# Hybrid encoder trunk on one core: zero-filled 128-row second score product in chunked attention, latent attention's chunk mask as four contraction rows, and a new layout for the experts' last third

## The chip, the cores and the metric

The kernel runs on one core of one Trainium2 chip. The metric is device time in microseconds for one execution of the whole program; the time before is the median of 3 runs. TensorE is called PE, VectorE DVE, ScalarE ACT, GpSimd POOL and SyncE SP.

## The reference, cut to what matters

Two layers on 512 tokens of width 1024, all in float32. Each layer mixes four branches (a state space scan, forgetting attention "fox", latent attention "mla", chunked attention "chk"), then a dense feed-forward (layer 0) or top-2-of-8 experts (layer 1), then a gated side input.

```
# mla: a query sees all keys of its own and earlier chunks of 64
mask = (kpos // 64) <= (qpos // 64)
s = where(mask, q @ k, -inf); prob = softmax(s)          # q, k: 64 plain + 32 rotary columns per head
# chk: own chunk and 8 chunks before it, plus a bias by clipped relative position
s = q @ k + bias; prob = softmax(s)                       # 64 columns per head
# experts: for each token the two best of 8
y = (silu(x @ w1[e]) * (x @ w3[e])) @ w2[e]               # 1024 -> 1408 -> 1024
```

## The kernel before, in words

Most products keep float32 precision by splitting each operand into a high and a low part: three PE products (hi·hi, hi·lo, lo·hi; lines 157 to 159, called L15x below) take the place of one. Weights are fetched by SP, split by ACT (line 137) and DVE (line 139), and used.

In the two mixers a planner orders the instructions of each engine by its own model of costs: large gate products (`gates`) fill PE while the softmax chains of the attention units run on DVE and ACT. Each unit does two heads `a`, and for each head four blocks `b` of 128 queries against n = 128(b+1) keys (`attention`, line 580): the score products (line 587), for fox a mask product of bf16 (line 589), for mla a mask product of one row (line 591), then maximum, exponential, scaling (lines 598 to 601), transposes (line 604) and products with the values (line 616). Tiles of one tag share a number of buffers; a new tile takes any that has come free.

- chk (`unit_chk`): `dq` holds a head's query, high part in its own 64 rows and low part in the other 64; `dk` holds the key's high part in both halves. Their product over 128 rows gives hi·hi + lo·hi. The second product, `dl` (the key's low part, 64 rows) with the high half of `dq`, adds hi·lo. This pair is issued 8 times for each n over two layers, two units and two heads, 32 in all.
- mla (`unit_mla`): the query `mq` and key `mk` are plain float32 tiles of 96 rows; each score product is two PE passes. Blocks mask the last 64 keys for the first 64 queries with the one-row product (32 of these). Four products of 64 rows (line 840) per layer add a low part of the query projection: 8 in all. POOL copies the rotary key into `mk` (line 855).
- s5_prep, between the two chk units, gives POOL a long chain of small operations (lines 357 to 448); POOL also adds the gated branches into `A` (line 669).

The experts (`moe`) have an order written out by hand for PE, ACT and DVE. Each expert has up to 128 rows in part A and the rest in part B. A works on split weights (`cut`, lines 1304 and 1306; products on line 1353). B uses the raw float32 weights with the rows as the stationary operand (line 1357); it is behind two branches on the count (lines 1491 and 1494): 64 rows, 32 rows or none. Weights come in 35 pieces an expert: up 0 to 27 in thirds i = 0, 1, 2 (the last third is 384 wide, the others 512), down in between and at 28 to 34. For 32 rows and i < 2, `quads` splits a piece's columns into four groups of 32 array columns that run side by side; for i = 2 only two groups run. `evac` gates a third, `turn` transposes it, `put` stores a part's output. Before the last expert stands a branch (line 1714) over `extras`, which holds a loop for experts with more than 192 rows.

## Time and profile before

| what | value |
|---|---|
| median of 3 runs | 2002.85 us (1998.05 to 2003.78) |
| profiled execution | 2003.2 us, span 2001.4 us |
[...]
| PE busy | 1941.3 us (97%) |
| DVE, ACT, POOL busy | 1191.4, 908.8, 315.6 us |
| DMA | 309.23 MB |

The span is from the first to the last instruction; 1.8 us of the profiled execution lie around it. A busy PE includes time in which a product's tail runs while nothing new is streamed, so what an edit on PE is worth is read from the starts of successive products and not from the busy share. A timeline row gives start, duration, engine, line, operation, tiles and shape (contraction rows * stationary columns, then rows x streamed columns), and in brackets the idle time ahead of it.

### The profile page before, as it was taken

What the parts mean: (1) busy time and instruction counts of PE and PEld (TensorE: products, weight loads), DVE (VectorE), ACT (ScalarE), POOL (GpSimd) and SP (SyncE); (2) the same over time, 40 slices, a digit from 0 to 9 for tenths busy, and PEclk for the clock granted to TensorE, in tenths of its full rate; (3) what the DMA queues carried; (4) which work ended last, traced back from release to release, by engine and by line L of the source; (5) the groups of instructions that cost most, each with busy time, mean ns of one, the idle gap of its engine ahead of it and who ended that gap; (6) DMA issues with size and microseconds to landing.
All of it is one profiled execution on the core that took longest, in us unless ns stands there. A gap on an engine that the chain in (4) does not pass through costs nothing. (4 is left out here: it accounts for less than half of the span.)

```text
span 2001.4 us, 27201 instructions
## 1 busy us (share of the span) xinstructions
PE 1941.3 (97%) x9922; PEld 1522.6 (76%) x9922; DVE 1191.4 (60%) x1849; ACT 908.8 (45%) x1345; POOL 315.6 (16%) x616
## 2 busy tenths in 40 slices
PE   7999999999999999999999999999999999999998
PEld 7787776788888888888777776887677877666567
DVE  5867564744333333345667564745899986566574
ACT  5535434333322223255435434333678776555454
POOL 1058020220000000001068020220100000000011
PEclk9999999999999999999999999999999999999999
DMA  5332223224433333323332223135699995858542
GB/s 170 119 107 85 75 89 132 67 92 159 147 95 95 102 98 90 111 89 110 99 106 85 76 89 132 53 112 213 230 365 373 372 353 214 299 205 316 198 156 106
DMA packets 94563, 309.23 MB, mean 155 GB/s; under 512 B 12161, under 2 KB 15105, under 8 KB 94402
## 3 DMA queue, kind: packets, MB, share of 16 engines
q1 hardware_dynamic: 89218, 289.40, 42.1%
q0 software_dynamic: 5040, 17.44, 2.6%
q8 instruction: 99, 1.62, 0.3%
q14 instruction: 62, 0.51, 0.1%
q10 hardware_dynamic: 144, 0.26, 0.0%
HBM read 283.46 MB, written 23.60 MB: 153 GB/s over the span
## 5 line engine op out<-in xcount | busy, mean ns | idle before, releaser
L137 ACT ACTIVATE whi<-wraw 128x1024 fp32r<-128x1024 f32 (+2 forms) x211 | 217.5, 1033 | 465.7 <-PE a L158 268.1
L139 DVE TENSOR_TENSOR wlo<-wraw,whi 128x1024 fp32r<-128x1024 f32 (+2 forms) x211 | 258.1, 1229 | 284.7 <-ACT whi L137 275.9
L158 PE MATMUL a<-hT_lo,whi 128*128 128x512 f32 (+3 forms) x1056 | 412.1, 391 | 0.8 <-DVE hT_lo L163 0.7
L159 PE MATMUL a<-hT_hi,wlo 128*128 128x512 f32 (+3 forms) x1056 | 412.5, 391 | 0.3 <-DVE wlo L139 0.3
L157 PE MATMUL a<-hT_hi,whi 128*128 128x512 f32 (+3 forms) x1056 | 411.8, 391 | 0.7 <-ACT hT_hi L163 0.7
L1306 DVE TENSOR_TENSOR wlo<-raw,whi 128x1024 fp32r<-128x1024 f32 (+1 forms) x198 | 228.0, 1160 | 52.3 <-ACT whi L1304 43.0
L159 PEld LDWEIGHTS a<-hT_hi,wlo 128*128 128x128 f32 (+1 forms) x1056 | 197.2, 187 | 42.8 <-issue 3.5
L158 PEld LDWEIGHTS a<-hT_lo,whi 128*128 128x128 f32 (+1 forms) x1056 | 197.5, 187 | 41.9 <-DVE hT_lo L163 1.9
L157 PEld LDWEIGHTS a<-hT_hi,whi 128*128 128x128 f32 (+1 forms) x1056 | 197.0, 187 | 41.6 <-issue 1.8
L1304 ACT ACTIVATE whi<-raw 128x1024 fp32r<-128x1024 f32 (+1 forms) x198 | 198.8, 1008 | 57.1 <-PE a L1353 39.5
L669 POOL TENSOR_TENSOR A<-A,t 128x512 f32<-128x512 f32 x48 | 78.2, 1660 | 262.3 <-DVE t L668 262.3
L157 PE MATMUL a<-whi,hT_hi 128*128 128x256 f32 (+2 forms) x328 | 110.6, 337 | 1.0 <-ACT hT_hi L163 1.0
L159 PE MATMUL a<-whi,hT_lo 128*128 128x256 f32 (+2 forms) x328 | 109.2, 334 | 0.3
L158 PE MATMUL a<-wlo,hT_hi 128*128 128x256 f32 (+2 forms) x328 | 108.8, 332 | 0.0
L1353 PE MATMUL a<-whi,heA_hi 128*128 128x512 f32 (+1 forms) x304 | 93.2, 388 | 9.5 <-PEq L1714 3.5
L1353 PE MATMUL a<-whi,heA_lo 128*128 128x512 f32 (+1 forms) x304 | 90.7, 379 | 0.0
L1353 PE MATMUL a<-wlo,heA_hi 128*128 128x512 f32 (+1 forms) x304 | 90.5, 378 | 0.0
L1353 PEld LDWEIGHTS a<-whi,heA_hi 128*128 128x128 f32 x304 | 54.4, 189 | 28.2 <-issue 13.9
L157 PEld LDWEIGHTS a<-whi,hT_hi 128*128 128x128 f32 x328 | 62.7, 191 | 7.3 <-ACT hT_hi L163 1.5
L159 PEld LDWEIGHTS a<-whi,hT_lo 128*128 128x128 f32 x328 | 62.7, 191 | 6.2 <-DVE hT_lo L163 0.9
L1306 DVE TENSOR_TENSOR r_lo<-raw,r_hi 128x1024 fp32r<-128x1024 f32 (+1 forms) x50 | 57.4, 1148 | 16.3 <-ACT r_hi L1304 13.9
L599 ACT ACTIVATE P<-b,mx 128x128 f32<-128x128 f32 (+1 forms) x64 | 33.7, 527 | 72.7 <-DVE mx L598 72.2
(529 smaller groups left out, 3562.5 us busy)
## 6 DMA issues: line engine op xcount, KB each, us to landing
raw<-in_moe_w13a SPq DMA_DIRECT2D x113, 512.0 KB, 7.3
raw<-in_moe_w SPq DMA_DIRECT2D x74, 512.0 KB, 8.1
wraw<-in_w_gate SPq DMA_DIRECT2D x64, 512.0 KB, 3.6
wraw<-in_ffn_w SPq DMA_DIRECT2D x64, 512.0 KB, 3.6
raw<-in_moe_w13b SPq DMA_DIRECT2D x61, 384.0 KB, 6.2
wraw<-in_w_in_T SPq DMA_DIRECT2D x20, 512.0 KB, 3.8
wraw<-in_w_branch SPq DMA_DIRECT2D x16, 512.0 KB, 3.7
wraw<-in_w_o SPq DMA_DIRECT2D x16, 512.0 KB, 3.6
```

Of the source, the lines that this page charges most:

```text
L137: act(hi[:, :n], raw[:, :n], AF.Copy)
L139: tt(out=lo[:, :n], in0=raw[:, :n], in1=hi[:, :n].bitcast(F), op=OP.subtract)
L157: mm(o, a[0], b[0], start=start, stop=False)
L158: mm(o, a[0], b[1], start=False, stop=False)
L159: mm(o, a[1], b[0], start=False, stop=stop)
L599: act(P[:, :n], src[:, :n], AF.Exp, bias=mx[:, 0:1], accum_out=mx[:, 1:2])
L669: gtt(out=A[m], in0=A[m], in1=g[m], op=OP.add)
L1304: act(hi[:, :w], raw[:, :w], AF.Copy)
L1306: return tt(out=lo[:, :w], in0=raw[:, :w], in1=hi[:, :w].bitcast(F), op=OP.subtract)
L1353: mm(dst[x][:, :w_], st[sa][:, k, :], w[:, cs[x]], start=first and q == 0, stop=last and q == 2)
```

## The change

The chk low key becomes one 128-row tile per head, zero in the half that faces the query's low part; the second product runs over 128 rows. POOL fills the zeros. The mla mask becomes four more contraction rows (96 to 100), loaded from a small table by POOL's DMA queue; the mask product and its two constant tiles go. The 64-row product in the mla projection runs over 128 rows. A pad takes the place of the constant tiles; another one of 128 bytes a partition is put in the router's pool.

In the experts `quads` holds for i = 2 too, which needs w2's rows of the last third in another order (set on the host), a gating in two pieces for the other row counts (`ordered`) and another transpose for 32 rows. Expert 6 does all of its last B pieces (28 to 34) ahead of A's 32 to 34. Its stores move from POOL's queue to SP's, and the DMAs of `extras` from SP's to POOL's.

```diff
-                    mm(s[:, :n], qT[:, qs], kT[:, :n], start=(i == 0), stop=(kind == "chk" and i == len(qk) - 1))
+                    mm(s[:, :n], qT[:, qs], kT[:, :n], start=(i == 0), stop=(kind != "fox" and i == len(qk) - 1))
-                if kind == "mla":
-                    mm(s[:, n - 64:n], half_b, neg_b, start=False, stop=True)
...
-                q2 = [qk_tile(cp, f"dq{a}", 9) for a in range(2)]
+                q2 = [qk_tile(cp, f"dq{a}", 10) for a in range(2)]
...
-                kl = qk_tile(cp, "dl", 9)
+                kl = [qk_tile(cp, f"dl{a}", 10) for a in range(2)]
+                for a in range(2):
+                    nc.gpsimd.memset(kl[a][halves(a)[1]].bitcast(F), 0.0)
...
-                        marks.append(tt(out=kl[own], in0=ps[own], in1=k2[a][own].bitcast(F), op=OP.subtract))
+                        marks.append(tt(out=kl[a][own], in0=ps[own], in1=k2[a][own].bitcast(F), op=OP.subtract))
...
-                    qks.append([(q2[a], k2[a]), (q2[a][own], kl[own])])
+                    qks.append([(q2[a], k2[a]), (q2[a], kl[a])])
...
+                for a in range(2):
+                    nc.gpsimd.dma_start(out=qs[a][96:100], in_=I["mla_mask"][0])
+                    nc.gpsimd.dma_start(out=ks[a][96:100], in_=I["mla_mask"][1])
...
-                    mm(ps, wuq[1][0:64, 1, ws], cqb[0:64], start=False, stop=True)
+                    mm(ps, wuq[1][:, 1, ws], cqb, start=False, stop=True)
...
-                attention(ap, "mla", [[(qs[a][0:96], ks[a][0:96])] for a in range(2)], V, (2 * pr, 2 * pr + 1), yps)
+                attention(ap, "mla", [[(qs[a][0:100], ks[a][0:100])] for a in range(2)], V, (2 * pr, 2 * pr + 1), yps)
...
-            return m == 32 and i < 2
+            return m == 32
...
+        def ordered(out, in0, in1):
+            a0, a1 = (x.rearrange("p (a b) -> p a b", a=2) for x in (in0, in1))
+            for q, lo, hi in ((out[:, 0:256], 0, 128), (out[:, 256:384], 128, 192)):
+                tt(out=q.rearrange("p (a b) -> p a b", a=2), in0=a0[:, :, lo:hi], in1=a1[:, :, lo:hi], op=OP.mult)
...
+            if quads(m, i) and i == 2:
+                for f, (c0, c1) in enumerate(((0, 128), (128, 192), (64, 192))):
+                    nc.tensor.transpose(bank[0:c1 - c0, f * 64:(f + 1) * 64], t_[0][0:64, c0:c1], ident[0:64, 0:64])
+                act(g[:, 0:2, 0:32], bank[:, 0:64].rearrange("p (k q) -> p k q", k=2), AF.Copy)
+                act(g[0:64, 2, 0:32], bank[0:64, 64:96], AF.Copy)
+                act(g[64:128, 2, 0:32], bank[64:128, 160:192], AF.Copy)
+                return
...
-            B(28, 32, 2)
+            ahead = er is None and e == NE - 2
+            B(28, 35 if ahead else 32, 2)
             A(32, 33, 34)
             if er is None and not last:
-                put(yd[e * 128:(e + 1) * 128, :], 128, nc.gpsimd if e == NE - 2 else nc.sync)
-            B(32, 35)
+                put(yd[e * 128:(e + 1) * 128, :], 128, nc.sync)
+            if not ahead:
+                B(32, 35)
...
+    blk = np.arange(S)[None, :] // 64 - 2 * np.arange(4)[:, None]
+    o["mla_mask"] = C(np.stack([blk == 0, NEG * (blk == 1)]).astype(np.float32))
```

## Rows read from the trace of the kernel before

**Rows 1.** The page, part 1: busy time of each engine.

```profile
PE 1941.3 (97%) x9922; PEld 1522.6 (76%) x9922; DVE 1191.4 (60%) x1849; ACT 908.8 (45%) x1345; POOL 315.6 (16%) x616
```

**Rows 2.** Waits of PE: us in total, times, longest.

```profile
PE b L604 <- DVE P L601: 7.9, 11, 1.8
```

**Rows 3.** Busy time by stretch, experts 4 to 6.

```profile
1640.00:1850.00 210.00, 207.92 (x1331) 142.87 (x1329) 134.03 (x135) 120.97 (x149) 5.13 (x5) 1.00 0.71 261
```

**Rows 4.** Timeline of PE, a chk block of 512 keys.

```profile
76.72 0.49 PE L604 MATMUL b<-cst,P 128*128 128x128 f32 x3
...
77.37 0.50 PE L587 MATMUL b<-dl,dq 64*128 64x512 f32 x1
77.80 0.50 PE L159 MATMUL a<-hT_hi,wlo 128*128 128x512 f32 x1
78.13 0.40 PE L157 MATMUL a<-hT_hi,whi 128*128 128x512 f32 x1
```

**Rows 5.** Timeline of PE, a fox block of 512 keys.

```profile
193.21 0.55 PE L604 MATMUL b<-cst,P 128*128 128x128 f32 x3
...
193.83 0.40 PE L587 MATMUL b<-f1s,f0s 128*128 128x512 f32 x1
194.07 0.23 PE L589 MATMUL b<-caus_b,ident_b 128*128 128x128 bf16 x1
...
194.43 0.40 PE L159 MATMUL a<-hT_hi,wlo 128*128 128x512 f32 x1
```

**Rows 6.** Timeline of PE, mla blocks and the gate products behind one.

```profile
277.94 0.49 PE L587 MATMUL b<-mk,mq 96*128 96x128 f32 x2
...
288.10 1.02 PE L587 MATMUL b<-mk,mq 96*128 96x512 f32 x2
289.05 0.20 PE L591 MATMUL b<-neg_b,half_b 1*128 1x64 bf16 x1
289.18 0.50 PE L158 MATMUL a<-hT_lo,whi 128*128 128x512 f32 x1
289.52 0.40 PE L159 MATMUL a<-hT_hi,wlo 128*128 128x512 f32 x1
...
292.49 0.39 PE L157 MATMUL a<-hT_hi,whi 128*128 128x512 f32 x1
```

**Rows 7.** Timeline of PE, the mla projection around line 840.

```profile
275.66 0.39 PE L839 MATMUL a<-cqb,whi 128*128 128x512 f32 x1
...
276.74 0.39 PE L158 MATMUL a<-cqa,whi 128*128 128x512 f32 x1
```

**Rows 8.** Part B, 32 rows: group of i = 2, then timeline, a piece of i = 0.

```profile
L1357 PE MATMUL b<-raw,yh 128*32 128x384 f32 x64 | 10.7, 488 | 0.0
...
1641.40 3.66 PE L1357 MATMUL b<-raw,yh 128*32 128x256 f32 x64
```

**Rows 9.** PE's branches: timeline, lines 1494 and 1714, and what waited.

```profile
1677.99 5.36 PE L1357 MATMUL b<-raw,yh 128*32 128x384 f32 x32
...
L1494 PEldq COMPARE_BRANCH  x1: 179/179/179, 1680.0 to 1680.0; - x1
...
L1714 PEldq COMPARE_BRANCH  x1: 4372/4372/4372, 1847.9 to 1847.9; - x1
...
1852.62 0.70 PE L1353 MATMUL a<-whi,heA_hi 128*128 128x512 f32 x2 [3.49 <-PEq L1714]
```

**Rows 10.** POOL: timeline, then a DMA's issue (ns) and landing (us).

```profile
118.39 0.46 POOL L359 TENSOR_TENSOR Qr<-gp,gp 128x128 f32<-128x128 f32 x1 [56.99 <-PE b L376]
...
261.87 11.03 POOL L669 TENSOR_TENSOR A<-A,t 128x512 f32<-128x512 f32 x8 [58.42 <-DVE t L668]
...
289.19 1.28 POOL L855 COPY mk<-krot 32x512 f32<-32x512 f32 x2 [14.08 <-DVE wlo L139]
...
L410 POOL DMA_DIRECT2D s5d<-Qr x4: 601/632/827, 128.8 to 1050.0; - x4
...
s5d<-Qr POOLq DMA_DIRECT2D x4, 256.0 KB, 2.4
```

## The prediction

> **What bounds the kernel now.** I read the page's first part, then the waits of PE, then the busy time by stretch, then PE's timeline around each place that the change touches. The first shows PE busy for 97% of the span [rows 1]; the reader is to see that no other engine passes 60%. A busy share alone doesn't say that PE is the limit, so the second view is needed: in the attention blocks PE's transposes wait for the softmax chain in 11 places only, 7.9 us in all [rows 2], and there are 96 such blocks (three kinds, two layers, two units, two heads, four blocks). In 85 of 96 the chain is ready before PE comes to it. The third view says the same of experts 4 to 6, where part B runs: PE is busy 207.92 of 210 us at a DMA share of 0.71 [rows 3]. So in the stretches that the change edits, time taken from PE is time taken from the span, if nothing new is waited for. The timelines then say how much there is to take: the distance from the start of one product to the start of the next is what a product costs.

> **The unit of account.** In a run of gate products of 128 rows and 512 columns, 13 distances take 292.49 - 289.52 = 2.97 us, so one product costs 0.228 us [rows 6].

> **chk's second product, 32 of them.** In the block of 512 keys the 64-row product takes 0.43 us to the next start and the gate product behind it 0.33 [rows 4]. Two products at 0.228 would be 0.46, so 0.30 us is lost where the array goes from 64 rows back to 128. The whole sequence, transposes to the second gate product, is 78.13 - 76.72 = 1.41 us. The fox block has the same transposes, two score products of 512 columns and a mask product besides, and takes 194.43 - 193.21 = 1.22 [rows 5]; there the second score product has 128 rows and costs 0.24. So chk's pair after the change can't well cost more than fox's with its mask: the saving is at least 0.19 a block. At most it is 0.40: the 0.30 above and 0.10 for the first product, if it too gets rid of what the switch to 64 rows costs it. I take 0.33, near the upper end, since fox's remainder holds a mask product that chk hasn't got. Blocks of 256 and 384 keys repeat the pattern; those of 128 are so short that loading the weights may set their pace, and for them I take 0.25 between 0.1 and 0.33, an estimate. Sum: 24 x 0.33 + 8 x 0.25 = 9.9 us (5.4 to 12.2).

> The wider product itself costs nothing more: the time goes by columns streamed, 0.24 us for fox's 128 rows against 0.43 for these 64 [rows 4, 5].

> **mla's mask, 32 of them.** Two score passes of 512 columns, the mask and the gate product behind it take 289.52 - 288.10 = 1.42 us; the mask's own distance is 0.13, the gate product's 0.34 instead of 0.228 [rows 6]. After the change two passes and a gate product are left. Plain float32 goes at 5.36 us for 16 turns of 384 columns on part B [rows 9], 0.87 ns a column, so the two passes are 0.89 and the sum 1.12: 0.30 us saved. If the product of 100 rows still delays its 128-row neighbour, only the mask and the 0.11 behind it go: 0.24. If the passes run without any gap, 0.34. In 6 of the 32 the mask stands behind value products and only its own 0.13 goes. Sum: 26 x 0.30 + 6 x 0.13 = 8.6 us (7.0 to 9.6).

> No row here has 100 rows, and the nearest, 96, leaves open whether it counts as the full array. [...]

> **The projection, 8 products.** From the product ahead of the 64-row one to the second behind it is 276.74 - 275.66 = 1.08 us for three [rows 7], against 3 x 0.228 = 0.69. Full 128 rows give back 0.39 each, 3.1 us in all; as with chk I keep half as the lower bound (1.6 to 3.2).

> **Experts, last third with 32 rows.** The group of i = 2 holds 64 instructions of 384 columns, 10.7 us [rows 8], in bunches of 32 [rows 9]: two experts, 5.36 us each. In four groups of columns there will be 64 instructions of 192. A bunch of 64 with 256 columns takes 3.66 us [rows 8]; if columns set that, 192 take 2.75 and 2.6 us are saved, if the number of instructions does, 3.66 and 1.7. Since 32 instructions of 384 and 64 of 256 cost the same by the column and group (0.87 and 0.89 ns), columns set it. Two experts: 5.2, less 0.2 for wider transposes, 5.0 us (3.4 to 5.2). The two more copies on ACT and the second gating operation on DVE have pieces 28 to 31 of B and A between them and their reader; without that cover they would cost under 1 us an expert.

> **Expert 6's order.** PE's branch over `extras` takes 4.37 us from 1847.9, and the first product of expert 7 has been waited for 3.49 us [rows 9]: little array work was queued ahead of it, B's last 24 short products. After the change A's 18 products of 0.228 us, 4.1 us, stand ahead. Does PE's sequencer run that far ahead? At 1680.0 it is at a branch while the bunch in the array goes on to 1677.99 + 5.36 = 1683.35 [rows 9]: 3.3 us, or some 20 products of 5.36 / 32. So most of the 4.37 is covered; I take 2.8 us saved (0 to 3.5).

> [...]

> **What is added, and what covers it.** POOL's eight zero fills: no row has this shape; the nearest are the addition of 1.4 us on 128 x 512 (11.03 / 8) and nothing [rows 10]. In the second chk unit a fill waits until the first head of the first unit has read its query, since its buffer comes free there; behind it on POOL is s5_prep's chain, which stands still anyway, 57 us up to 118.39 [rows 10]. That new tiles take whatever buffer is free shows in mla: both copies into the second unit's keys run together at 289.19, right behind the first head's last scores, the second head's still to come [rows 6, 10]. I take 0; without the cover 8 x 1.4 = 11 us.

> The mask rows are four DMAs a unit on POOL, 0.63 us to issue and 2.4 to land [rows 10]. At worst they queue behind the additions that end at 261.87 + 11.03 = 272.90: issued by 275.4, landed by 277.8, the rotary copies done by 276.7, beside a first score at 277.94 [rows 6, 10]. I take 0; if the score comes a microsecond earlier, under 1 us a layer. POOL waits 58 us ahead of those additions, so the DMAs can go long before. SP's two stores of expert 6 hold up the fetches of expert 7 by ACT's and DVE's copies, a microsecond or two, and 18 buffers are ahead; POOL, whose gathers of the last expert stand behind these stores, is freed of issuing them. The loads of `extras` aren't run: expert 7's first product follows the branch. The pads issue nothing.

> **Sum.** The mixers give 9.9 + 8.6 + 3.1 = 21.6 us, of which I count nine tenths, 85 blocks of 96 not waiting for the chain: 19.4. The experts give 5.0 + 2.8 = 7.8. Together 27.2 us, against the profiled 2003.2 us (span 2001.4 and 1.8 around it): 1976.0; from the median, 2002.85, which is 0.35 below: 1975.7. I predict 1976 us, own range 1969 (33.7 saved, every upper bound) to 1987 (16 saved: 14.0 x 0.9 + 3.4). Less than 0.3%, 6 us, can't be told from no change.

> **Rivals.**
> - The lost time belongs to the change of kind (transposes, scores, gates) and not to the number of rows. For it: fox, with no 64-row product, loses some too [rows 5]. Against it: the projection has one kind only and loses 0.39 [rows 7]. Then chk and the projection give nothing, mla 32 x 0.13 = 4.2, the experts 7.8: 1991. Chance 0.13.
> - The softmax chain takes it back: PE reaches the transposes sooner and waits. For it the 11 waits, against it the 85 blocks without [rows 2]. A third of 21.6 and the experts' 7.8 are 15.0: 1988. Chance 0.07.
> - The first rival, and with it the experts stay at their bounds (3.4, branch 0), and the mask rows cost a microsecond or two: 4.2 + 3.4 - 1.5 = 6.1, 1997, no change. Chance 0.07.
> - Slower: the planner puts the second unit's zero fills behind s5_prep's chain on POOL. The chain goes on from 118.39 to 261.87 - 58.42 = 203.45 [rows 10], and PE, whose order is fixed, stands at the second product of unit two: 85 us, in both layers 170, less 27: 2146. It decides whether the fill is queued ahead of the operation that waits until 118.39. Against it: POOL is free when the buffer comes free. Chance 0.07.
> - The forecast: 0.66.

> Range 1966 to 1993: it takes in the first two rivals, and 3 us below for a plan that happens to fit better. Faster by over 0.3%: 0.66 + 0.13 + 0.07 = 0.86; the same 0.07; slower 0.07.

> **What would show it.** In the new trace the block of 512 keys in chk should take about 1.08 us where 1.41 stood, dl and the gate product behind it 0.23 to 0.25 each; mla's two passes and a gate product about 1.12; the three projection products 0.69; part B's i = 2 bunch of 64 about 2.75 us; the wait at line 1714's branch under 1 us. PE's waits for P should stay near 8 us. The prediction is wrong if dl still takes 0.4 us, if PE waits for a fill or for the mask's DMA, or if the blocks keep their distance and the waits ahead of the transposes grow by what the products gave.

## The result, and the profile after

The changed kernel takes 1956.85 us (median of five runs, 1956.64 to 1960.47) where the kernel before takes 2002.79 on the same chip (1998.05 to 2003.78): a ratio of 0.9781, 95% interval 0.9767 to 0.9794, 45.9 us faster. The prediction was 1976 (1966 to 1993): the sign was right, the gain too small by 19 us. The profiled span went from 2001.4 to 1955.2 us.

Read first what was to show each step. The page of the changed kernel, part 1: PE is busy for 97% of a shorter span, as in [rows 1].

```profile
PE 1903.8 (97%) x9954; PEld 1511.0 (77%) x9954; DVE 1186.8 (61%) x1859; ACT 908.1 (46%) x1349; POOL 332.7 (17%) x632
```

PE's timeline of the changed kernel: a chk block of 512 keys, one projection, an mla block of 512 keys, the 32-row pieces of expert 4's last third.

```profile
75.65 0.53 PE L599 MATMUL b<-cst,P 128*128 128x128 f32 x3
75.94 0.47 PE L584 MATMUL b<-dk,dq 128*128 128x512 f32 x1
76.25 0.39 PE L584 MATMUL b<-dl,dq 128*128 128x512 f32 x1
76.47 0.39 PE L159 MATMUL a<-hT_hi,wlo 128*128 128x512 f32 x1
76.70 0.40 PE L157 MATMUL a<-hT_hi,whi 128*128 128x512 f32 x1
...
269.66 0.39 PE L838 MATMUL a<-cqb,whi 128*128 128x512 f32 x1
269.89 0.39 PE L839 MATMUL a<-cqb,wlo 128*128 128x512 f32 x1
270.11 0.39 PE L157 MATMUL a<-cqa,whi 128*128 128x512 f32 x1
270.34 0.39 PE L158 MATMUL a<-cqa,whi 128*128 128x512 f32 x1
...
281.90 1.02 PE L584 MATMUL b<-mk,mq 100*128 100x512 f32 x2
282.36 0.80 PE L158 MATMUL a<-hT_lo,whi 128*128 128x512 f32 x1
283.00 0.40 PE L159 MATMUL a<-hT_hi,wlo 128*128 128x512 f32 x1
...
1645.22 2.81 PE L1357 MATMUL b<-raw,yh 128*32 128x192 f32 x64
1647.95 0.73 PE L1353 MATMUL b<-whi,gA_hi 128*128 128x512 f32 x2
```

The chk block takes 76.70 - 75.65 = 1.05 us (1.08 forecast, 1.41 before [rows 4]); dl and the gate product behind it take 0.22 and 0.23. The mla passes and a gate product take 283.00 - 281.90 = 1.10 (1.12 forecast). The projection's three products take 0.68 (0.69 forecast), and the bunch of 64 products takes 2.73 (2.75 forecast). In these places the prices worked out by hand hold to some hundredths of a microsecond. So the missing 19 us are, for the most part, not in the products.

The waits of PE in the changed kernel, those for the softmax chain and at the branch over the extra experts (us, times, longest):

```profile
PE b L599 <- DVE P L596: 6.9, 13, 1.2
PE a L1353 <- DVEq L1730: 1.8, 1, 1.8
```

The first is near the 7.9 of [rows 2]: the chain takes nothing back. The second was forecast at under 1 us; what it waits for is no longer PE's own branch (PEq, 3.49 us in [rows 9]) but DVE's (DVEq). The zero fills last 0.52 us each and the mask's transfers land after 1.9; PE waits for neither.

Then the whole by landmarks: the start of PE's first row of each kind, in microseconds. The last four columns belong to the experiments below.

| PE's first ... | before | after | chk alone | mask alone | projection alone | experts alone |
|---|---|---|---|---|---|---|
| mla score, layer 0 | 277.9 | 271.8 | 272.7 | 277.9 | 276.6 | 278.6 |
| s5 product, layer 0 | 346.1 | 333.6 | 340.6 | 339.5 | 345.1 | 346.8 |
| s5 GLU, layer 0 | 411.7 | 398.4 | 407.4 | 404.2 | 413.6 | 412.4 |
| chk score, layer 1 | 959.8 | 946.7 | 955.4 | 952.6 | 961.6 | 960.5 |
| s5 product, layer 1 | 1246.4 | 1220.5 | 1235.6 | 1231.6 | 1246.3 | 1246.2 |
| s5 GLU, layer 1 | 1314.8 | 1285.5 | 1304.0 | 1295.5 | 1314.7 | 1313.0 |
| product of expert 0 | 1417.8 | 1387.6 | 1406.3 | 1398.0 | 1417.1 | 1415.1 |
| product of the merge | 1937.0 | 1890.3 | 1925.9 | 1911.6 | 1936.6 | 1917.8 |
| end of the span | 2001.4 | 1955.2 | 1990.0 | 1976.9 | 2001.0 | 1981.8 |

Up to expert 0 the change saves 30.2 us (19.4 forecast), in the experts 16.5 (7.8 forecast). Both halves are short by about ten.

What the prediction had not read is a set of stops. The waits of PE in the kernel before:

```profile
PE b L511 <- DVE zr L502: 4.1, 2, 2.0
PE a L1353 <- issue: 3.2, 1, 3.2
PE b L475 <- DVE U L468: 1.5, 4, 0.5
PE b L475 <- ACT U L468: 1.4, 2, 0.7
```

and stretches of the kernel before, around s5's two stages in layer 1 and behind the branch (columns: from and to, length, busy time of PE, PEld, DVE, ACT and POOL, granted clock, DMA share, GB/s):

```profile
1246.00:1254.00 8.00, 6.53 (x36) 5.84 (x35) 3.10 (x9) 2.13 (x4) 1.15 (x2) 0.79 0.55 219
1274.00:1282.00 8.00, 6.02 (x24) 5.03 (x25) 8.00 (x10) 1.28 (x1) 5.40 (x3) 0.79 0.00 0
1851.00:1862.00 11.00, 6.17 (x19) 4.53 (x20) 2.58 (x3) 3.06 (x3) 1.58 (x4) 0.69 0.50 185
```

and the changed kernel's at the same work:

```profile
1219.00:1227.00 8.00, 7.06 (x47) 6.05 (x46) 3.98 (x9) 3.40 (x5) 2.12 (x2) 1.00 1.01 390
1248.00:1256.00 8.00, 7.42 (x38) 6.17 (x37) 7.32 (x9) 0.00 (x0) 8.00 (x6) 1.00 0.10 17
1809.00:1820.00 11.00, 9.20 (x41) 7.31 (x41) 6.83 (x7) 6.08 (x7) 0.00 (x0) 1.00 0.84 266
```

PE stood 4.1 us for zr, 2.9 for U, 3.2 for nothing that the profile names; around these stops the granted clock was 0.50 of full for part of the stretch, from 1249.7 to 1253.1, 1277.0 to 1280.4 and 1853.9 to 1860.7 us; (1 - clock) x length, the time's worth of full clock that was lost, is 1.7, 1.7 and 3.4 us. A fourth such stretch, 0.50 from 1102.9 to 1106.4 and so 1.7 us lost, is behind the 1.8 us wait for P of [rows 2]. In the changed kernel the clock is 1.00 until the last 7 us. The means over the profiled executions are 0.995 before and 0.998 after.

Counted directly, PE's waits of over 0.15 us up to expert 0 sum to 36.3 us before and 31.2 after, and the lost clock there to 5.1 and 0: 10.2 of the 30.2 us are not products.

### The profile page after: what moved, and what is told of

Same layout as the page of the kernel before. It is cut to its first block, busy times and chain, and to the rows that moved or that the text cites. A ratio compares the mean times of both kernels' runs of the same rounds, so it can differ in the third digit from the quotient of the medians.

```text
span 1955.2 us, 27356 instructions
## 1 busy us (share of the span) xinstructions
PE 1903.8 (97%) x9954; PEld 1511.0 (77%) x9954; DVE 1186.8 (61%) x1859; ACT 908.1 (46%) x1349; POOL 332.7 (17%) x632
## 5 line engine op out<-in xcount | busy, mean ns | idle before, releaser
L1226 POOL DMA_INDIRECT xa<-hd,TI x8 | 12.4, 1553 | 319.0 <-PE a L1326 310.8
```

The source lines that it names most:

```text
L1226: return nc.gpsimd.indirect_dma_start(out=xg, out_offset=None, in_=src, in_offset=bass.IndirectOffsetOnAxis(ap=idx, axis=0))
```

## The experiments

Each was timed against the kernel before on the same chip. Experts' durations run from one expert's first product to the next one's (expert 7: to the merge's first).

**The parts, one by one.** Each kernel is the kernel before with one part of the change.

```diff
+                    nc.gpsimd.memset(kl[a][halves(a)[1]].bitcast(F), 0.0)
+                    qks.append([(q2[a], k2[a]), (q2[a], kl[a])])
```

```diff
-                    mm(s[:, n - 64:n], half_b, neg_b, start=False, stop=True)
+                    nc.gpsimd.dma_start(out=qs[a][96:100], in_=I["mla_mask"][0])
+                    nc.gpsimd.dma_start(out=ks[a][96:100], in_=I["mla_mask"][1])
```

```diff
-                    mm(ps, wuq[1][0:64, 1, ws], cqb[0:64], start=False, stop=True)
+                    mm(ps, wuq[1][:, 1, ws], cqb, start=False, stop=True)
```

The fourth takes all of the diff that concerns the experts, the pad and the queues included.

> The kernel before with chk's second score product on 128 rows, nothing else changed. Theory (the row count of the product is the cost; the extra gain over the sum comes from stops of PE and stretches at half clock, above all around the s5 stage): in the two traces the 32 blocks' score products and the product behind them fall by 11.5 us, so about 1991 us, with the wait for zr ahead of line 511 (2.0 us a layer) and the half-clock stretches of layer 1 left as they are. Rival (any shorter PE stream makes the planner choose another order, and the stops around s5 go with it): 1984 us or less, the wait for zr gone. Rival (the change of kind costs, not the rows): 2002, no change.

> The kernel before with mla's mask as four more rows, nothing else changed. Theory: the products give 8.8 us and, as the mla stretch lies right ahead of s5 in PE's order, the waits for U and zr shrink too: 1990 to 1994 with the products alone, 1983 to 1987 with the s5 stops and their half-clock stretches in layer 1 gone. Rival (the stops go only with the whole change's order): 1994, wait for zr still 2.0 us a layer. Rival (only the mask product's own 0.13 us goes, the float32 passes keep their neighbours late): 1998.

> The kernel before with the projection's third product on 128 rows instead of 64, nothing else changed. Theory (rows): 8 products, 0.2 to 0.4 us each: 1999.7 to 2001. Rival (a new order from the planner counts for more than the products): outside 1999 to 2003, with other waits around s5. Rival (kind): no change, 2002.8.

> The kernel before with the experts' part alone (quads for i = 2, expert 6's order, the queues), attention as it was. Theory: this half doesn't hang on the mixers, so it gives what the stretch from layer 1's end to the end of the kernel gave in the whole change: 16 us, 1987, with the stop of 3.2 us behind line 1714's branch and the half-clock stretch at 1852 to 1861 gone. Rival (the prediction's price: 5.0 for the quads and 2.8 for the branch): 1995.

Measured: chk 0.9948 (0.9935 to 0.9961), mask 0.9891 (0.9877 to 0.9906), projection 0.9997 (0.9988 to 1.0005), experts 0.9904 (0.9890 to 0.9919). chk gives its products, 11.4 us of span, and leaves the stops. The projection's products give 0.41 us each in six of eight (the three distances from the product ahead of each to the second behind it go from 1.10 to 0.69); in the last of each layer the first mla score then waits 0.3 us, so 2.2 in all, less than the spread of the runs. The mask gives far more than its products: 19.8 us before expert 0, and 5.6 in experts whose code it doesn't touch. By the ratios the four parts add to 52 us (0.0260 of 2002), the whole is 44: mask and experts each remove the same stop behind the branch, some 5 us, and the rest lies within the intervals.

**The mask without its replacement.**

```diff
-                if kind == "mla":
-                    mm(s[:, n - 64:n], half_b, neg_b, start=False, stop=True)
```

> The kernel before without mla's mask product and without anything in its place (mla's mask is left out), 96 rows as before. Theory (the mask product goes, and with it both what it cost and the order that left s5 short of cover; the four rows are only its replacement): as with the mask as rows, 1979 to 1981, 23 gate triples instead of 19 ahead of s5's second stage, no wait for zr, clock at 1.00 until the end. Rival (the new order comes with the rows' transfers): 19 triples, the wait for zr of 2.0 us a layer stays, 1992.

Other attention results send tokens elsewhere and an extra expert runs, so the total, 1.043, says nothing. Up to expert 0 it is the test: 22.2 us saved there against 19.8 with the mask as rows, 23 triples in place of 19, no wait for zr. The rows themselves cost some 2 us by this; the rest is what the absence of the product does.

**Why s5 is late.** DVE's timeline of the kernel before, layer 0, up to the first step of s5's chain (`zr`):

```profile
355.06 1.23 DVE L139 TENSOR_TENSOR wlo<-wraw,whi 128x1024 fp32r<-128x1024 f32 x1 [6.05 <-ACT whi L137]
356.20 1.28 DVE L487 TENSOR_TENSOR zr<-sd,b 128x512 f32<-128x512 f32 x2
```

and of the changed kernel:

```profile
335.38 1.23 DVE L139 TENSOR_TENSOR wlo<-wraw,whi 128x1024 fp32r<-128x1024 f32 x1
341.06 1.28 DVE L484 TENSOR_TENSOR zr<-sd,b 128x512 f32<-128x512 f32 x2 [4.46 <-DMA sd<-s5d]
```

Before, the split of a weight (`wlo`) stands on DVE ahead of the chain and waits 6.05 us for ACT's half of it. The chain begins 4.4 us after s5's first products end (351.8) and its zr comes 2.0 us after PE asks for it. After, the same kind of split finds its weight ready, DVE is idle before the chain, and the chain begins 2.8 us after those products (338.3); from those products to s5's second stage PE then has 24.4 us of other work where it had 19.9. Two attempts to get that cover in the kernel before, without the mask's edit:

```diff
-            g = gates(0, ring, between={1: scan, 5: scan})
+            g = gates(0, ring, between={2: scan, 5: scan})
```

```diff
-                    mm(o, M[:, aa, :], U4[:, aa, :], start=True, stop=False)
+                    with tc.issue_after(late[0].ins) if aa == 0 else nullcontext():
+                        mm(o, M[:, aa, :], U4[:, aa, :], start=True, stop=False)
```

> The kernel before with s5's second stage issued one gate later (behind gate 2 of the last eight instead of gate 1), attention as it was. Theory (the mask's edit moved four gate triples from mla's stretch to the cover of s5's chain, 19 to 23 triples, and so ended the wait for zr; more cover without the mask's edit must do the same): wait for zr gone in both layers, 4.1 us, with the half-clock stretch at 1276 to 1281 another 1.7: 1996. The other half-clock stretch of layer 1, at 1248, stays. Rival (the wait for zr is the planner's and only moves, or what it covered is waited for later): 2000 to 2003.

> The kernel before with one order edge on PE: the first product of s5's second stage is queued behind the fourth gate triple of the last eight gates, so product 2 and some 28 triples stand ahead of it instead of 19; all products are as before. Theory (lack of cover for s5's chain of some 22 us makes the wait): no wait for zr, 4.1 us in both layers, and the half-clock stretch of 1.7 us behind it in one layer: 1996. Expert 7's second stop stays. Rival (what the wait covered is waited for later, at the gates or the products): 2000 to 2002.

Neither gained: 1.0001 (0.9992 to 1.0010) and 1.0011 (1.0002 to 1.0020). In the first the planner kept s5's second stage where it was, 19 triples and the wait for zr included. The second does end the wait for zr, but the waits of PE now show

```profile
PE a L157 <- DVE t L673: 5.7, 2, 2.9
PE a L159 <- DVE wlo L139: 3.5, 2, 2.2
```

PE now stops for other work of the same late DVE. The theory that PE's cover alone was short falls. That DVE's earlier start is what made the difference fits the rows above, but no run sets it by itself: it came with the order which the planner chose once the mask products were gone, and which of its decisions does it wasn't isolated.

**The pad.** One line, 128 bytes a partition; in the second kernel half of it, [128, 16].

```diff
         nc.gpsimd.memset(zero, 0)
+        rt.tile([128, 32], F, name="gap")
```

> The kernel before with the one line of the pad in the experts' pool (128 bytes a partition, never read or written), nothing else. Theory (where the tiles behind the pad lie in SBUF sets the pace of part A): in the two traces part A's products of 512 columns start 0.232 us apart before and 0.227 after, and experts 1, 2, 3 and 5, whose work is the same, are 0.6 us shorter each; so about 0.6 us for each of eight experts, 4 to 5 us, about 1997, with 50.6 us instead of 51.25 for experts 1 to 3. Rival (the prediction: a pad issues nothing and is worth nothing; the 0.6 us comes from the moved transfers): 2002, experts at 51.25.

> The kernel before with a pad of 64 bytes instead of 128 in the experts' pool: the tiles behind it then start 192 bytes past a multiple of 256, where they started 128 past it before and on it with the whole pad. Theory (an operand has to start on a multiple of 256 bytes): no gain, experts 1 to 3 at 51.25 us, 2001 to 2002. Rival (any other place than 128 past is as good, or half a step brings half): 50.6 to 50.9, 1997 to 1999.

Measured: 0.9973 (0.9964 to 0.9983) and 0.9989 (0.9980 to 0.9998). Timelines of expert 1, the kernel before:

```profile
1477.81 0.63 PE L1353 MATMUL a<-whi,heA_hi 128*128 128x512 f32 x2
1478.27 0.63 PE L1353 MATMUL a<-wlo,heA_hi 128*128 128x512 f32 x2
1478.74 0.63 PE L1353 MATMUL a<-whi,heA_lo 128*128 128x512 f32 x2
1479.21 0.63 PE L1353 MATMUL a<-r_hi,heA_hi 128*128 128x512 f32 x2
```

and with the whole pad:

```profile
1473.77 0.62 PE L1354 MATMUL a<-whi,heA_hi 128*128 128x512 f32 x2
1474.23 0.62 PE L1354 MATMUL a<-wlo,heA_hi 128*128 128x512 f32 x2
1474.68 0.61 PE L1354 MATMUL a<-whi,heA_lo 128*128 128x512 f32 x2
1475.13 0.62 PE L1354 MATMUL a<-r_hi,heA_hi 128*128 128x512 f32 x2
```

A pair starts every 0.467 us before and every 0.453 with the pad, 0.233 and 0.227 a product. Experts 1 to 3 take 51.25 us before, 50.60 with the pad (the changed kernel: 50.6) and 50.95 with half of it; from expert 0 to the merge the pad saves 519.2 - 514.3 = 4.9 us. In the programs' memory layout the tiles behind the pad start 128 bytes past a multiple of 256 before, on one with the pad, 192 past one with half of it. So the pad's place is worth the 4 to 5 us that were expected, and the theory that only a multiple of 256 helps falls: half a step brings about half. Which of the tiles behind the pad matters stays open.

**The branch behind expert 6.** The second stop of the kernel before, on PE:

```profile
1853.64 0.84 PE L1353 MATMUL a<-whi,heA_lo 128*128 128x512 f32 x2
1857.68 1.22 PE L1353 MATMUL a<-whi,heA_hi 128*128 128x512 f32 x2 [3.20 <-issue]
1858.69 1.05 PE L1353 MATMUL a<-wlo,heA_hi 128*128 128x512 f32 x2
```

Six products after the branch PE waits for nothing that a row names, then runs at about half its pace (0.9 to 1.0 us a pair where 0.47 is usual, at the clock of 0.50 up to 1860.7). The page's part 3 counts 99 loads of code on queue q8 (kind "instruction"), 1.62 MB in all, 16 KB each; with the mask alone there are 98, in the changed kernel 100. From 580.9 to 811.7 us of the kernel before, eight of these loads start, and PE does 1019 products and 1018 weight loads: 255 instructions of PE a load, near the 256 that the expectations take for a block. In the packets of this queue one such load runs from 1855.42 to 1856.36, in the middle of the stop, and PE goes on 1.3 us after its end. All seven profiled kernels with the 9922 PE products of [rows 1] have such a second stop, of 2.4 to 3.7 us (the kernel before, chk alone, projection alone, both pads, both s5 attempts); in each, PE goes on 1.3 to 1.5 us after the end of such a load. The edits: 48, 35 or 32 products of one element at the start, which only move the code (the three kernels with shift in their name); expert 6's old order (the two with no_ahead); the old queues.

```diff
     start_norm(N)
+    tiny = bank_b()
+    for _ in range(48):
+        mm(tiny[0:1, 0:1], cst[0:1, 0:1], cst[0:1, 0:1], start=True, stop=True)
...
-            ahead = er is None and e == NE - 2
+            ahead = False
...
-                put(yd[e * 128:(e + 1) * 128, :], 128, nc.sync)
+                put(yd[e * 128:(e + 1) * 128, :], 128, nc.gpsimd if e == NE - 2 else nc.sync)
...
-            nc.gpsimd.dma_start(out=ie_d, in_=iel)
+            nc.sync.dma_start(out=ie_d, in_=iel)
```

> The kernel before with 48 products of one element each added at the start, where PE still waits for the first rows (192 instructions on PE's stream, nothing reads their result). Theory (PE's second stop behind the branch over the extra experts, 3.2 us with a half-clock stretch, hangs on where the code behind the jump lies against the 256-instruction blocks in which it is loaded; without the mask products it lay 65 instructions earlier, and 192 more bring it to the same place modulo 256): the second stop goes, expert 7 takes 79.5 to 80.5 us instead of 84.4, and the kernel with more work is faster, 1996 to 1999 where before has 2001 to 2002. Rival (the second stop is of the queues or of the mask's edit): expert 7 at 84.4, 2002 or a microsecond more for the added products.

> The changed kernel with expert 6's part B in the old order (its pieces 32 to 34 behind A's). Theory (the order covers only part of PE's branch; the rest of what the experts gained there was the second stop and the half-clock stretch behind it, which the kernel with the mask alone also lost without touching the experts): PE's stop at the branch goes from 1.8 to 3.1 to 3.5 us, 1958.5 with no second stop; 1963 if the second stop of 3.2 us and the half-clock stretch are back. Prediction's price: 2.8 us, 1959.6.

> The changed kernel with expert 6's stores and the extra experts' transfers on the queues of the kernel before. Theory (the queues give nothing: with the mask alone, ACT waited 4.5 us for SP at this branch and PE didn't): 1956 to 1958, PE's stop at the branch 1.8 us, no second stop, though ACT waits for SP again. Rival (SP's part in the branch held expert 7's first cuts and so PE): 1960 to 1962, a second stop of some 3 us behind the branch.

> The changed kernel with 35 products of one element each added at the start (139 instructions on PE's stream; nothing reads their result), which brings the code behind the branch over the extra experts to where it lay in the kernel before, modulo 256 instructions. Theory (the code's place decides on the second stop): a second stop of 2.4 to 3.6 us for nothing that the profile shows, a half-clock stretch behind it, expert 7 at 82 to 84.5 us instead of 78.6: 1961 to 1964 with the added products' 2 us at the start. Rival (the changed kernel has no second stop because of its order or queues): expert 7 at 78.6, 1957 to 1959.

> The changed kernel with expert 6's part B in the old order and 32 products of one element added at the start, so that the code behind the branch lies as in the kernel before, modulo 256 instructions. Theory (either the code's place or the order that has A's 18 products run while the code is loaded suffices to avoid the second stop; with neither it must return): a second stop of 2.4 to 3.6 us, expert 7 at 82 to 84.5 us, 1963 to 1967. Rival (the queues of the change avoid it): expert 7 at 78.7, 1960 to 1962.

| kernel | ratio (interval) | expert 6 | expert 7 | PE's stops at the branch |
|---|---|---|---|---|
| before | 1 | 72.55 | 84.36 | 3.49, then 3.20 |
| before_gap | 0.9973 (0.9964 to 0.9983) | 72.06 | 83.34 | 3.6, then 2.4 |
| mask_only | 0.9891 (0.9877 to 0.9906) | 72.10 | 79.25 | 3.05 |
| before_shift | 0.9991 (0.9979 to 1.0003) | 72.25 | 79.32 | 3.15 |
| experts_only | 0.9904 (0.9890 to 0.9919) | 67.58 | 78.66 | 1.8 |
| after | 0.9781 (0.9767 to 0.9794) | 67.58 | 78.63 | 1.80 |
| after_no_ahead | 0.9792 (0.9779 to 0.9805) | 68.54 | 78.66 | 2.6 |
| after_old_queues | 0.9781 (0.9769 to 0.9794) | 68.96 | 78.63 | 3.2 |
| after_shift | 0.9794 (0.9779 to 0.9808) | 67.59 | 78.97 | 1.8 |
| no_ahead_shift | 0.9792 (0.9776 to 0.9809) | 66.67 | 80.45 | 0.7, then 1.5 for ACT |

PE's timeline of the kernel before with the 48 products added:

```profile
1855.06 0.71 PE L1353 MATMUL a<-whi,heA_hi 128*128 128x512 f32 x2 [3.15 <-PEq L1714]
1855.61 0.62 PE L1353 MATMUL a<-wlo,heA_hi 128*128 128x512 f32 x2
1856.07 0.63 PE L1353 MATMUL a<-whi,heA_lo 128*128 128x512 f32 x2
1856.54 0.64 PE L1353 MATMUL a<-whi,heA_hi 128*128 128x512 f32 x2
```

Adding work took the second stop and its half-clock stretch away, 5.0 us of expert 7, against 2.7 that the products cost at the start; the total, 0.9991, isn't clear of noise. The code load behind the branch is still there (1858.08 to 1859.00), and PE runs through it without a stop. So by this run the 3.20 us stop of the kernel before hangs on where the code lies; that PE waits there for the load itself is an inference from their times. The rule of the expectations, the place modulo 256 by the count of instructions, failed. With the new order (after_shift) the changed kernel doesn't stop again: there the second load had ended at 1815.21, before PE's first product of expert 7 at 1816.25, where in the kernel before it ended 3.7 us behind that product. Without it (no_ahead_shift) a stop of 1.5 us came back, and expert 7 took 80.45 us, less than the 82 expected; that load ended at 1816.71 and PE went on at 1818.11, but the profile puts this stop down to ACT, whose cut ended at 1817.79, so its cause isn't shown. What sets the time of the second load stays open. The new order and the new queues have a small effect by expert 6's duration, 1.0 and 1.4 us; the ratios (0.9792 and 0.9781 against 0.9781) can't tell it. With the old queues PE's stop at the branch is 3.2 us and not the 1.8 expected.

**Rows of mla.** Queries (and keys alike) get 28 rows of zeros more.

```diff
-                    nc.gpsimd.dma_start(out=qs[a][96:100], in_=I["mla_mask"][0])
+                    nc.gpsimd.dma_start(out=qs[a][96:128], in_=I["mla_mask"][0])
```

> The changed kernel with mla's queries and keys filled to 128 rows: the mask's transfers bring 32 rows, 28 of them zero, instead of 4. Theory A (a product of less than 128 rows delays its 128-row neighbour): the gate product behind mla's scores falls from 0.32 us and more to 0.23, 0.1 us for 32 blocks: 3 us less, 1954. Theory B (the delay goes with the change from float32 to split products, whatever the rows; the 100-row product already counts as the full array): the same 1957, the product behind at 0.32.

Measured 0.9780 (0.9767 to 0.9794), as the changed kernel. PE's timeline of the block of 512 keys:

```profile
281.97 1.02 PE L584 MATMUL b<-mk,mq 128*128 128x512 f32 x2
282.43 0.79 PE L158 MATMUL a<-hT_lo,whi 128*128 128x512 f32 x1
283.06 0.40 PE L159 MATMUL a<-hT_hi,wlo 128*128 128x512 f32 x1
```

The passes and the gate product take 1.09 us with 128 rows and 1.10 with 100: neither theory's 0.32 shows here. The gate product's distance is 0.63 us because its start is recorded at 282.43, while the row of the two passes runs to 282.99; the sum is what two passes at 0.87 ns a column and one product at 0.228 us make (1.12). So a product of 100 rows costs its neighbour no more than one of 128, and neither delays it.

## Why the prediction was wrong

**Right.** The products. chk's blocks gave 11.5 us by PE's start-to-start distances where 9.9 stood in the sum: 0.39 to 0.40 a block of 256 to 512 keys and 0.29 in six of the eight of 128 (0.17 in the two whose first product stands apart), since the first product gains 0.10 too (0.33 and 0.25 were taken; the upper bound of 12.2 was the better choice). mla gave 8.8 (8.6), the projection 2.2 (3.1: in the last product of each layer the gain is waited away), the quads 5.1 (5.0). Together 27.6 against 26.6; that the sum is this close is in part luck, since chk came out 1.6 above its term and the projection 0.9 below. The covers named for the zero fills and the mask's transfers held, PE waits for neither. The rival that the change of kind costs falls with the projection's 0.41 a product and dl's 0.22; the rivals of the softmax chain and of the zero fills fall with PE's waits.

**Wrong, first: "The pads issue nothing."** True, and yet the pad is worth 4.9 us, because it moves all tiles behind it. The prediction read the pad's instructions and not its place.

**Wrong, second: the factor of nine tenths on the mixers.** It took 2.2 us off for new waits. Instead, waits went: of the 30.2 us up to expert 0 22.5 are products by their distances, and the 7.7 left are stops of PE, above all for s5's zr and U, and half-clock stretches, less what new small waits took (counted directly, waits and lost clock are 10.2; the two counts don't close by 2.5). With the mask alone it is 11.0 (19.8 - 8.8). The lost clock, 5.1 us of this, is in part luck of the execution that was profiled: with the same waits for zr and U, the kernel with the pad lost 3.4 us there and the one with the experts' part alone 1.7. The prediction read PE's waits for P only, since that is the line it feared, and left the other lines of the same view as they were. The mask's edit is what ended the waits for zr, as mask_only and before_no_mask show; that it did so through the planner's order on DVE is argued from the rows, and which decision of the planner it was stays open.

**Wrong, third: the branch, 2.8 us.** Experts 6 and 7 together went from 156.9 to 146.2 us; without the quads (2.6) and the pad (1.2) that is 6.9. The step asked how far the products issued ahead cover the branch's 4.37 us. That cover held: PE's branch runs from 1805.5 to 1809.4 and its products to 1809.9. But the first stop went only from 3.49 to 1.80 us, 1.7 saved where 2.8 stood, since expert 7's first product then waits for a cut behind DVE's branch, which DVE reaches at 1809.9 and the step left out. It did not ask what the second stop, 5 us later in the same timeline, was, nor price the clock behind it. The order itself is worth 1.0 us; the queues, priced at nothing, 1.4. The second stop and its clock, some 5 us, went with the change; in the kernel before, moving the code alone removes them.

The differences are 4.9 for the pad, 9.9 for the factor and the stops (2.2 + 7.7), 4.1 for the branch and 1.0 for the products: 19.9, against 46.2 - 27.2 = 19.0 of the spans.

## What to carry to other kernels

Price each stop of the stretch that an edit shortens, not only the wait that the edit might lengthen, and with each stop the granted clock of the 10 us behind it (here 0.50 for 3.4 to 6.8 us). A pad, a tile's size or a constant that goes is an edit of every address behind it, and instructions that go move all code behind them: where a change has such lines, forecast a few microseconds either way (here 4.9 us by the pad, 5.0 of expert 7 by moved code), or hold place and code fixed to measure the rest. Product distances from the timeline gave the sum here to 4%, its single terms to between 2% (mla, quads) and 40% (the projection).

## What the hardware showed that was not expected

```profile
346.00:354.00 8.00, 6.53 (x43) 5.59 (x42) 2.88 (x8) 1.91 (x4) 1.15 (x2) 1.00 0.50 199
372.00:380.00 8.00, 5.96 (x29) 4.42 (x29) 8.00 (x10) 1.28 (x1) 5.27 (x3) 1.00 0.00 0
```

and with the pad, which changes nothing there, it is layer 0 whose clock falls, to a mean of 0.79 over 8 us, and layer 1 whose clock doesn't:

```profile
344.00:352.00 8.00, 6.52 (x36) 5.91 (x36) 2.65 (x7) 1.65 (x3) 1.15 (x2) 0.79 0.48 190
...
1270.00:1278.00 8.00, 5.96 (x29) 4.33 (x28) 8.00 (x9) 0.22 (x1) 5.12 (x3) 1.00 0.00 0
```

With the projection alone, whose waits for U and zr are the same, both layers fall:

```profile
345.00:353.00 8.00, 6.53 (x36) 5.91 (x35) 2.90 (x8) 1.90 (x3) 1.15 (x2) 0.79 0.56 198
1246.00:1254.00 8.00, 6.53 (x36) 5.79 (x36) 3.02 (x8) 2.04 (x4) 1.15 (x2) 0.79 0.53 212
```

So such a stop costs its length and, in some executions and not in others, 1.7 us more; what decides it, no run here shows.

- 192 instructions of nothing at the start made expert 7 5.0 us shorter, 1800 us later.
